# The last norm of a two-block transformer kernel: a shorter root, factors moved from GpSimd to VectorE, stores in four pieces

## Chip, core and metric

The kernel runs as one program on one core of a Trainium2 chip. The metric is the device time of one execution in microseconds; the median of three runs is compared. Engines are named as the profile names them: PE is TensorE (matmul), PEld its weight loads, DVE is VectorE, ACT is ScalarE, POOL is GpSimd, SP is SyncE, which here only issues transfers.

## What is computed

Two transformer blocks are applied to 256 tokens of width 1024, the first with two layers of attention, the second with a feed-forward net (ffn), a mixer, a second ffn, a gated projection and the last norm. Only the end matters here:

```python
h = h + 0.5 * swiglu(rms_norm_2(h, ffn2_norm[i]), ffn2_w_in[i], ffn2_w_out[i])
hn = rms_norm_2(h, ple_norm[i])
h = h + jax.nn.sigmoid(hn @ ple_w_gate[i]) * (p[i] @ ple_w_proj[i])
return rms_norm_2(h, final_norm)        # x * rsqrt(mean(x*x) + EPS) * g
```

## The kernel before

All weights are one stream of chunks of 8 tiles of 128x128. SP loads a chunk into `wraw` (4 buffers; line 97), ACT rounds it into `whi` (line 108), DVE computes the rest `wlo` (line 115), and PE multiplies with both (line 86). The instructions of each engine stand in the order in which the program writes them; nothing reorders them at run time, so an instruction that waits holds up all that stand behind it on its engine. `tick` is called once a chunk: it starts the split of the chunk two ahead and lets side tasks take one step each.

A norm (`Norm.stats`) is such a side task. PE sums squares into a PSUM bank, POOL sets a small tile `nv` to 1.0 (line 354), DVE writes the mean squares into that same tile (line 361), takes a reciprocal root in 11 small instructions (lines 284 to 289), and PE spreads the result over the partitions (line 315, and line 86 for its last part). Since DVE's write comes after POOL's in the same tile, DVE waits for POOL. The norm in front of the second ffn is called `fstats`.

Between `fstats` being spawned and the second ffn the program makes pool `q4`, and SP loads the last norm's factors `gf` into it, one copy a partition (line 1582).

The last part takes the 1024 columns in cuts of 512, 256 and 256 (`PLE_CUT`), for two halves `i` of 128 tokens each. For each cut and half the generator `finals` multiplies by the gate (line 1619), adds the residual (line 1621), sums squares in ACT (line 1622) and multiplies by `gf` (line 1625): in DVE, but for the last cut of the second half in POOL. Then `rsqrt1` takes the root of one column of numbers by a bit trick (line 297) and three steps of two instructions (lines 299 and 300); after the second step of the first half's root DVE does the second half's gate and residual (`between`). The rows are then scaled by the root and stored: of the second half, ACT scales 384 columns (line 1674) and DVE 640 (line 1676), and each queue stores its part in one transfer (lines 1677 and 1678).

Of the kernel before, what the change touches and what calls it, by code (L numbers as in the profile page):

```python
# [14 lines left out]
AF = mybir.ActivationFunctionType  # L15
OP = mybir.AluOpType
# [7 lines left out]
P = 128  # L24
# [33 lines left out]
def hybrid_kernel(ctx: ExitStack, tc: tile.TileContext, wst, xt, pt, gains, c0, c1, c2, lmaskc, alpha, relb, rpb, gfin, out):  # L58
    nc = tc.nc
    V, S, G, PE = nc.vector, nc.scalar, nc.gpsimd, nc.tensor  # L60
# [6 lines left out]
    def nm(s):  # L67
        count[0] += 1
        return f"{s}_{count[0]}"

    def act(w=NT, dt=F32, p=P):

        assert w <= NT
        return sb.tile([P, TP], dt, tag="a", name=nm("a"), bufs=A_BUFS)[:p, :w]

    def til(shape, tag, bufs=1, dt=F32, pool=None):
        return (pool or sb).tile(shape, dt, tag=tag, name=nm(tag), bufs=bufs)

    def bank(tag):
        return ps.tile([P, 512], F32, tag=tag, name=nm(tag), bufs={"mm": 3, "at": 4, "st": 1}[tag])  # L80
# [120 lines left out]
    def finish(*names):  # L201
        while any(n not in done for n in names) or pending:
            tick()
# [36 lines left out]
    def proj(acts, n, evac, need=None, work=1):  # L240

        b = bank("mm")[:, :n]
        last = len(acts) - 1
        for k in range(last + 1):
            xh, xl = acts[k]
            wh, wl = weights(1)
            mm(b, wh, xh[:, :n], start=k == 0, stop=False)
            mm(b, wh, xl[:, :n], start=False, stop=False)
            mm(b, wl, xh[:, :n], start=False, stop=k == last)
            if k == last:  # L250
                pending.append([evac, b, need, work])
            used()

    def triple(b, hl, wts, i, first, last):

        t = slice(i * P, (i + 1) * P)
        mm(b, hl[0][:, t], wts[0], start=first, stop=False)
        mm(b, hl[1][:, t], wts[0], start=False, stop=False)
        mm(b, hl[0][:, t], wts[1], start=False, stop=last)

    def split(x, scale, n=NT, pool=None):

        if pool:
            hi, lo = til([P, n], "hid", 44, F32R, pool), til([P, n], "hid", 44, F32R, pool)
        else:
            hi, lo = act(n, F32R), act(n, F32R)
        split_into((hi, lo), x, scale)
        return hi, lo
# [24 lines left out]

    def rsqrt1(m, mh, between=()):

        y, t = til([P, 1], "nyf", 2, pool=q4), til([P, 1], "ntf", 2, pool=q4)
        V.tensor_scalar(y.bitcast(I32), m.bitcast(I32), -0.5, float(0x5F3759DF), op0=OP.mult, op1=OP.add)
        for k in range(3):
            V.scalar_tensor_tensor(t, y, mh, y, op0=OP.mult, op1=OP.mult)
            V.scalar_tensor_tensor(y, t, 1.5, y, op0=OP.add, op1=OP.mult)  # L300
            if k == 1:
                for f in between:
                    f()
        return y

    def bcast(cols, b, rows=False):
# [133 lines left out]
    norm = Norm(gn[:, G_NORM:], NT)  # L440
# [46 lines left out]
    for l in range(2):  # L487
        t = dr.tile([P, pitch], F32, name=f"rows{l}")
# [524 lines left out]
    nxt = Norm(gn[:, G_NORM + 8:], NT)  # L1013
# [3 lines left out]
    norm, nxt = nxt, Norm(g2, NR, gn[:, G_FIN1:])  # L1017
# [5 lines left out]
    norm, nxt = nxt, Norm(gn[:, G_MIX:], NR)  # L1023
# [11 lines left out]
    def ffn(norm, nxt, pad=0):  # L1035
        hl = norm.hl
        fs = ExitStack()
        q2 = fs.enter_context(tc.tile_pool(name=nm("q2"), bufs=1))
        if pad:
            til([P, pad], "padf", pool=q2)  # L1040
        hid, zs = [], []

        def ev_g(b):
            z = act(NR)
            V.tensor_tensor(z, b, norm.rb, op=OP.mult)  # L1045
            S.activation(z, z, AF.Silu)  # L1046
            zs.append(z)

        def ev_u(b):
            z = zs.pop(0)  # L1050
            V.tensor_tensor(z, b, z, op=OP.mult)  # L1051
            hid.append(split(z, 0.5, NR, q2))

        for j in range(22):
            proj(hl, NR, ev_g, norm.ready)
            proj(hl, NR, ev_u)
        for j in range(8):
            def ev(b, j=j):
                x = act(NR)
                V.tensor_tensor(x, b, norm.rb, op=OP.mult)  # L1060
                V.tensor_tensor(x, x, norm.xs[j], op=OP.add)  # L1061
                nxt.add(x)
            proj(hid, NR, ev)
        finish()
        fs.close()

    ffn(norm, nxt, 32)
    norm, nxt = nxt, Norm(gn[:, G_FFN2:], NR)
# [509 lines left out]
    norm, nxt = nxt, Norm(gn[:, G_PLE:], NR)  # L1578
    spawn("fstats", norm.stats(rows=True))
    q4 = ctx.enter_context(tc.tile_pool(name="q4", bufs=1))  # L1580
    gf = q4.tile([P, 1024], F32, name="gf")
    nc.sync.dma_start(gf, bass.AP(tensor=gfin.tensor, offset=gfin.offset, ap=[[0, P], [1, 1024]]))
    til([P, 32], "pad2")
    ffn(norm, nxt, 16)
    norm = nxt

    turned = [[bank("at") for _ in range(2)] for _ in range(2)]
# [23 lines left out]
    os_ = [til([P, 1024], "fo", 2, pool=q4) for _ in range(2)]  # L1611

    def finals(wp, i, c, o, w):
        b = bank("mm")[:, :w]
        for k in range(2):
            triple(b, phl[k], [x[:, k * w:(k + 1) * w] for x in wp], i, k == 0, k == 1)
        t = os_[i][:, o:o + w]
        yield
        V.scalar_tensor_tensor(t, t, 1.0, b, op0=OP.add, op1=OP.mult)
        yield  # L1620
        V.tensor_tensor(t, t, turned[i][o // 512][:, o % 512:o % 512 + w], op=OP.add)
        S.activation(til([P, 512], "fsq", 2, pool=q4)[:, :w], t, AF.Square, scale=1.0 / 32,
                     accum_out=su[:, 2 * c + i:2 * c + i + 1])
        yield
        (G if c == 2 and i else V).tensor_tensor(t, t, gf[:, o:o + w], op=OP.mult)  # L1625
        yield

    assert pos[0] == MOVED
    for c, (o, w) in enumerate(PLE_CUT):
        bs = [bank("mm")[:, :w] for _ in range(2)]  # L1630
        if c < 2:
            d = CH * P // w
            for k in range(0, 8, d):
                wts = [weights(w // P) for _ in range(d)]
                for i in range(2):
                    for j in range(d):
                        triple(bs[i], norm.hl[k + j], wts[j], i, k + j == 0, k + j == 7)
                used()
            if c == 0:
                finish("plestats", "turn")  # L1640
            for i in range(2):
                S.activation(os_[i][:, o:o + w], bs[i], AF.Tanh, scale=hr[:, i:i + 1])
            wp = weights(2 * w // P)
            fs = [finals(wp, i, c, o, w) for i in range(2)]
            for n in (1, 2):
                for f in fs:
                    for _ in range(n):
                        next(f)
            used()
            for f in fs:  # L1650
                next(f)
        else:
            V.scalar_tensor_tensor(sv, su[:, :2], EPS, su[:, 2:4], op0=OP.add, op1=OP.add)
            V.tensor_scalar(svh, sv, -0.5, None, op0=OP.mult)
            wts = [weights(w // P) for _ in range(8)]
            wp = weights(2 * w // P)
            fs = [finals(wp, i, c, o, w) for i in range(2)]
            for i in range(2):
                for k in range(8):
                    triple(bs[i], norm.hl[k], wts[k], i, k == 0, k == 7)  # L1660
                S.activation(os_[i][:, o:o + w], bs[i], AF.Tanh, scale=hr[:, i:i + 1])
                next(fs[i])
                if i == 0:
                    next(fs[0]), next(fs[0])
            for i in range(2):
                next(fs[i])
                v, vh = til([P, 1], "fv", 2), til([P, 1], "fvh", 2, pool=q4)
                V.tensor_tensor(v, sv[:, i:i + 1], su[:, 4 + i:5 + i], op=OP.add)
                V.scalar_tensor_tensor(vh, su[:, 4 + i:5 + i], -0.5, svh[:, i:i + 1], op0=OP.mult, op1=OP.add)
                r = rsqrt1(v, vh, () if i else [lambda: next(fs[1])] * 2)  # L1670
                t = slice(i * P, (i + 1) * P)
                cut = 384 if i else 512
                a, b = os_[i][:, :cut], os_[i][:, cut:]
                S.activation(a, a, AF.Copy, scale=r)
                if i:
                    V.tensor_scalar(b, b, r, None, op0=OP.mult)
                    S.dma_start(out[t, :cut], a)
                    nc.sync.dma_start(out[t, cut:], b)
                else:
                    nc.sync.dma_start(out[t, :cut], a)  # L1680
                    S.activation(b, b, AF.Copy, scale=r)
                    S.dma_start(out[t, cut:], b)
    assert pos[0] == n_chunk * CH, (pos[0], wst.shape)


# [152 lines left out]
```

## Time and profile before

| | |
|---|---|
| median of 3 runs | 1072.31 us (1071.44 to 1072.75) |
| the profiled execution's own time | 1072.28 us |
| its span in the trace | 1070.5 us |
| granted clock of TensorE over the span | 0.998 |
| PE busy | 1059.7 us (99%) |
| DVE busy | 796.4 us (74%) |
| ACT busy | 585.5 us (55%) |
| POOL busy | 53.9 us (5%) |

Times in the trace count from the start of the span. The execution's own time is 1.8 us longer than its span, and 0.03 us from the median. A matmul's row counts as busy while it is queued, so a PE of 99% says little of its speed; whether it is held up is read from the starts of its instructions.

### The profile page before, as it was taken

Reading aid. Unit: us, or ns where it says so; the run is one execution under the profiler, and the core shown is the slowest. Engines: PE = TensorE matmul, PEld = TensorE weight load, DVE = VectorE, ACT = ScalarE, POOL = GpSimd, SP = SyncE. Lnnn points to the kernel's source line nnn. Section 1 sums busy time; section 2 is a strip of 40 time slices with the busy share of each in tenths; the row PEclk is TensorE's granted clock in tenths of the full one; section 3 lists DMA queues with packets and bytes.
Section 4 is the critical chain, followed back from the end, with each engine's and each line's share of the span. In section 5 each row is a group of like instructions: output and inputs, shape, how many; then the busy total and the mean of one; then the engine's idle time right before and its main releaser. Section 6 shows DMA issues by size and latency. Waiting matters only on the chain.

```text
span 1070.5 us, 22921 instructions
## 1 busy us (share of the span) xinstructions
PE 1059.7 (99%) x9183; PEld 1020.9 (95%) x9183; DVE 796.4 (74%) x1646; ACT 585.5 (55%) x1035; POOL 53.9 (5%) x111
## 2 busy tenths in 40 slices
PE   9999999999999999999999999999999999999996
PEld 8999899999999999999999987999999999999996
DVE  7888867788887788766666659996687866666666
ACT  7356644544565466555545475777554655554444
POOL 3420002012000000000000200000000000000000
PEclk9999999999999999999999999999999999999999
DMA  8763345565434565655665535544455665556651
GB/s 291 230 209 120 121 137 167 188 171 180 150 122 137 172 192 166 207 195 195 196 212 186 189 130 178 178 139 139 138 183 194 208 189 195 196 197 197 200 175 59
DMA packets 71900, 188.08 MB, mean 176 GB/s; under 512 B 22745, under 2 KB 27353, under 8 KB 71794
## 3 DMA queue, kind: packets, MB, share of 16 engines
q1 hardware_dynamic: 71362, 186.12, 53.6%
q8 instruction: 72, 1.18, 0.5%
q10 hardware_dynamic: 432, 0.50, 0.1%
q14 instruction: 34, 0.28, 0.1%
HBM read 185.53 MB, written 3.65 MB: 177 GB/s over the span
## 4 chain that ended last, share of the span: by engine, by line
PE 92%; DVE 5%; DMA 1%; issue 1%; ACT 0%; SPq 0%; POOL 0%; DVEq 0%; ACTq 0%
PE mm L86 82%; PE at L86 7%; DVE wlo L115 2%; DMA wraw<-in_wst_dram 1%; PE at L752 1%; PE st L86 1%; DVE sc L1221 1%; DVE m L1220 0%; PE at L819 0%; PE st L315 0%; ACT whi L108 0%; PE at L820 0%; PE at L821 0%; DVE fo L1625 0%; SPq L431 0%
## 5 line engine op out<-in xcount | busy, mean ns | idle before, releaser
L86 PE MATMUL mm<-a,whi 128*128 128x256 f32 (+1 forms) x4192 | 747.1, 282 | 0.0
L86 PEld LDWEIGHTS mm<-a,whi 128*128 128x128 f32 x4192 | 637.7, 188 | 7.2 <-issue 5.6
L86 PE MATMUL mm<-a,wlo 128*128 128x256 f32 (+1 forms) x2096 | 585.2, 279 | 0.0
L115 DVE TENSOR_TENSOR wlo<-wraw,whi 128x1024 fp32r<-128x1024 f32 (+1 forms) x341 | 411.0, 1208 | 19.0 <-ACT whi L108 18.0
L86 PEld LDWEIGHTS mm<-a,wlo 128*128 128x128 f32 x2096 | 394.0, 188 | 0.0
L108 ACT ACTIVATE whi<-wraw 128x1024 fp32r<-128x1024 f32 (+1 forms) x341 | 354.5, 1042 | 67.6 <-PE mm L86 46.1
L86 PE MATMUL mm<-hid,whi 128*128 128x256 f32 x704 | 119.8, 276 | 0.0
L86 PEld LDWEIGHTS mm<-hid,whi 128*128 128x128 f32 x704 | 105.9, 188 | 0.0
L86 PE MATMUL mm<-hid,wlo 128*128 128x256 f32 x352 | 97.2, 276 | 0.0
L86 PEld LDWEIGHTS mm<-hid,wlo 128*128 128x128 f32 x352 | 66.1, 188 | 0.0
L1051 DVE TENSOR_TENSOR a<-mm,a 128x256 f32<-128x256 f32 x42 | 17.8, 424 | 46.4 <-PE mm L86 46.4
L271 ACT ACTIVATE hid<-a 128x256 fp32r<-128x256 f32 x44 | 18.5, 421 | 57.0 <-DVE a L1051 57.0
L86 PE MATMUL mm<-whi,a 128*128 128x512 f32 (+1 forms) x184 | 46.7, 346 | 0.0
L1046 ACT ACTIVATE a<-a 128x256 f32<-128x256 f32 x44 | 18.4, 418 | 49.5 <-DVE a L1045 49.4
L271 ACT ACTIVATE a<-a,gn 128x256 fp32r<-128x256 f32 (+1 forms) x40 | 20.6, 514 | 43.9 <-DVE a L1061 25.9
L1045 DVE TENSOR_TENSOR a<-mm,rb 128x256 f32<-128x256 f32 x42 | 17.8, 424 | 27.5 <-PE mm L86 27.5
L86 PEld LDWEIGHTS mm<-whi,a 128*128 128x128 f32 x184 | 31.0, 188 | 4.3 <-issue 0.3
L409 ACT ACTIVATE gate<-gate 128x272 f32<-128x272 f32 (+1 forms) x32 | 13.6, 424 | 38.8 <-DVE gate L408 38.8
L533 ACT ACTIVATE pra<-at,mx,hs 128x272 f32<-128x272 f32 x32 | 18.2, 573 | 28.6 <-DVE mx L700 28.6
L1060 DVE TENSOR_TENSOR a<-mm,rb 128x256 f32<-128x256 f32 x16 | 6.8, 425 | 34.4 <-PE mm L86 34.4
L86 PE MATMUL mm<-wlo,a 128*128 128x512 f32 (+1 forms) x92 | 31.5, 342 | 0.0
L271 ACT ACTIVATE a<-a 128x256 fp32r<-128x256 f32 (+1 forms) x24 | 10.1, 422 | 26.4 <-DVE a L1564 12.1
(339 smaller groups left out, 1030.7 us busy)
## 6 DMA issues: line engine op xcount, KB each, us to landing
wraw<-in_wst_dram SPq DMA_DIRECT2D x332, 512.0 KB, 3.7
bias<-rows SPq DMA_DIRECT2D x16, 160.0 KB, 4.3
rows<-in_rpb_dram SPq DMA_DIRECT2D x8, 316.0 KB, 5.3
wraw<-in_wst_dram SPq DMA_DIRECT2D x8, 256.0 KB, 4.4
a<-in_xt_dram SPq DMA_DIRECT2D x8, 136.0 KB, 4.3
big<-tb SPq DMA_DIRECT2D x2, 512.0 KB, 5.2
c<-in_c_dram SPq DMA_DIRECT2D x1, 512.0 KB, 4.3
gf<-in_gfin_dram SPq DMA_DIRECT2D x1, 512.0 KB, 4.7
```

Of the source, the lines that this page charges most:

```text
L86: PE.matmul(o, l, r, start=start, stop=stop)
L108: S.activation(his[c][:, s], raws[c][:, s], AF.Copy)
L115: V.tensor_tensor(los[c][:, s], raws[c][:, s], his[c][:, s].bitcast(F32), op=OP.subtract)
L271: S.activation(hl[0], x, AF.Copy, scale=scale)
L409: S.activation(t, t, AF.Tanh, scale=0.5)
L533: S.activation(outs[i], src, AF.Exp, bias=bias, scale=scale, accum_out=su[:, i:i + 1])
L752: PE.transpose(b[:, j * P:(j + 1) * P], pr[:, o:o + P], ident)
L1045: V.tensor_tensor(z, b, norm.rb, op=OP.mult)
L1046: S.activation(z, z, AF.Silu)
L1051: V.tensor_tensor(z, b, z, op=OP.mult)
L1060: V.tensor_tensor(x, b, norm.rb, op=OP.mult)
L1221: V.match_replace(sc[:, w], m8, sc[:, w], TAKEN)
```

## The change

The root of the last norm takes one step of third order (three instructions on the column) and one of second order (two) in place of three of second order. Both new steps leave out a constant factor, 1.5 and 2.25, together 3.375, so POOL multiplies `gf` by 3.375 once, ahead of the second ffn. The last cut of the second half is no longer multiplied by `gf` in POOL: DVE does it together with the scaling by the root. The second half is scaled and stored in four pieces: 256 columns by DVE with the factors and 384 by DVE without, both stored from SP's queue, and twice 192 by ACT, stored from ACT's queue. A pad of 16 numbers in the ffn's pool goes; the new small tile `nuf` takes the room, and no other tile has another address.

```diff
     def rsqrt1(m, mh, between=()):
-        y, t = til([P, 1], "nyf", 2, pool=q4), til([P, 1], "ntf", 2, pool=q4)
+        y, t, u = [til([P, 1], f"n{c}f", 2, pool=q4) for c in "ytu"]
         V.tensor_scalar(y.bitcast(I32), m.bitcast(I32), -0.5, float(0x5F3759DF), op0=OP.mult, op1=OP.add)
-        for k in range(3):
-            V.scalar_tensor_tensor(t, y, mh, y, op0=OP.mult, op1=OP.mult)
-            V.scalar_tensor_tensor(y, t, 1.5, y, op0=OP.add, op1=OP.mult)
-            if k == 1:
-                for f in between:
-                    f()
+        V.scalar_tensor_tensor(t, y, mh, y, op0=OP.mult, op1=OP.mult)
+        V.scalar_tensor_tensor(u, t, 5 / 3, t, op0=OP.add, op1=OP.mult)
+
+        V.scalar_tensor_tensor(y, u, 1.25, y, op0=OP.add, op1=OP.mult)
+        for f in between:
+            f()
+        V.scalar_tensor_tensor(t, y, mh, y, op0=OP.mult, op1=OP.mult)
+        V.scalar_tensor_tensor(y, t, 2 / 3, y, op0=OP.add, op1=OP.mult)
         return y
...
     til([P, 32], "pad2")
-    ffn(norm, nxt, 16)
+    G.tensor_scalar(gf, gf, 3.375, None, op0=OP.mult)
+    ffn(norm, nxt)
...
-        (G if c == 2 and i else V).tensor_tensor(t, t, gf[:, o:o + w], op=OP.mult)
+        if c < 2 or i == 0:
+            V.tensor_tensor(t, t, gf[:, o:o + w], op=OP.mult)
...
-                cut = 384 if i else 512
-                a, b = os_[i][:, :cut], os_[i][:, cut:]
-                S.activation(a, a, AF.Copy, scale=r)
+                x = os_[i]
                 if i:
-                    V.tensor_scalar(b, b, r, None, op0=OP.mult)
-                    S.dma_start(out[t, :cut], a)
-                    nc.sync.dma_start(out[t, cut:], b)
+                    V.scalar_tensor_tensor(x[:, o:], x[:, o:], r, gf[:, o:], op0=OP.mult, op1=OP.mult)
+                    nc.sync.dma_start(out[t, o:], x[:, o:])
+                    V.tensor_scalar(x[:, 384:o], x[:, 384:o], r, None, op0=OP.mult)
+                    nc.sync.dma_start(out[t, 384:o], x[:, 384:o])
+                    for s in (slice(0, 192), slice(192, 384)):
+                        S.activation(x[:, s], x[:, s], AF.Copy, scale=r)
+                        S.dma_start(out[t, s], x[:, s])
```

The first place is POOL's queue from the mixer to the end. Here are its rows before, with what each waits for; `nv_11651` is the small tile of `fstats`, `nv_13966` that of the next norm, `fo_13950` the second half's rows.

```order
L1357 MEMSET big_8805 128x1024
L1109 CAST lmask_8159<-a_8157 128x192 [waits DMAHW1_49]
L354 MEMSET nv_11651 128x4
L354 MEMSET nv_13966 128x4 [waits DVE_49]
L1625 TENSOR_TENSOR fo_13950<-fo_13950,gf 128x256 [waits DMAHW3_49,DMAHW4_49,DMAHW0_49,DMAHW6_49,PE_49,DMAHW7_49,Activation_49,Pool_49]
```

And the same rows now (its line numbers are those of the changed kernel, here 3 higher).

```order
L1360 MEMSET big_8805 128x1024
L1112 CAST lmask_8159<-a_8157 128x192 [waits DMAHW1_49]
L1587 TENSOR_SCALAR gf<-gf 128x1024 [waits DMAHW3_49,DMAHW0_49,DMAHW4_49,DVE_49,DMAHW6_49,PE_49,DMAHW7_49,Activation_49,Pool_49]
L357 MEMSET nv_11651 128x4
L357 MEMSET nv_13966 128x4
```

The scaling of `gf`, which waits for the load of `gf` among others, now stands ahead of the MEMSET of the small tile of `fstats`, which waited for nothing; the multiplication at the end is gone.

The second place is DVE's queue at `fstats`, as it is now, with what each row waits for; its order is the same as before.

```order
L343 TENSOR_TENSOR sqacc_11327<-sqacc_11327,a_11606 128x256 [waits Activation_49]
L364 TENSOR_SCALAR nv_11651<-st_11650 128x2 [waits PE_49,Pool_49]
L284 TENSOR_SCALAR nyv_11658<-nv_11651 128x4 [waits DVE_49]
...
L289 SCALAR_TENSOR_TENSOR nyv_11658<-ntv_11659,nyv_11658 128x4 [waits DVE_49]
L115 TENSOR_TENSOR wlo_11672<-wraw_11490,whi_11655 128x1024 [waits DMAHW7_49,Activation_49]
L115 TENSOR_TENSOR wlo_11705<-wraw_11530,whi_11701 128x1024 [waits DMAHW0_49,Activation_49]
```

The first small instruction of `fstats` (line 361 before, 364 now) waits for PE's sums and for POOL's MEMSET, and two weight splits stand behind its root.

The third place is DVE's last instructions, the second half's root and scaling; before:

```order
L297 TENSOR_SCALAR nyf_14271<-fv_14267 128x1
L299 SCALAR_TENSOR_TENSOR ntf_14272<-nyf_14271,fvh_14268 128x1
L300 SCALAR_TENSOR_TENSOR nyf_14271<-ntf_14272,nyf_14271 128x1
L299 SCALAR_TENSOR_TENSOR ntf_14272<-nyf_14271,fvh_14268 128x1
L300 SCALAR_TENSOR_TENSOR nyf_14271<-ntf_14272,nyf_14271 128x1
L299 SCALAR_TENSOR_TENSOR ntf_14272<-nyf_14271,fvh_14268 128x1
L300 SCALAR_TENSOR_TENSOR nyf_14271<-ntf_14272,nyf_14271 128x1
L1676 TENSOR_SCALAR fo_13950<-fo_13950,nyf_14271 128x640
```

And now:

```order
L298 TENSOR_SCALAR nyf_14270<-fv_14266 128x1
L299 SCALAR_TENSOR_TENSOR ntf_14271<-nyf_14270,fvh_14267 128x1
L300 SCALAR_TENSOR_TENSOR nuf_14272<-ntf_14271 128x1
L302 SCALAR_TENSOR_TENSOR nyf_14270<-nuf_14272,nyf_14270 128x1
L305 SCALAR_TENSOR_TENSOR ntf_14271<-nyf_14270,fvh_14267 128x1
L306 SCALAR_TENSOR_TENSOR nyf_14270<-ntf_14271,nyf_14270 128x1
L1679 SCALAR_TENSOR_TENSOR fo_13950<-fo_13950,nyf_14270,gf 128x256
L1681 TENSOR_SCALAR fo_13950<-fo_13950,nyf_14270 128x384
```

Of the seven instructions of the root six are left, and the one scaling of 640 columns has become one of 256 with the factors and one of 384.

## Rows read from the trace of the kernel before

**Rows 1.** Page, parts 4 and 5: chain that ended last; weight loads, mean ns.

```profile
PE 92%; DVE 5%; DMA 1%; issue 1%; ACT 0%; SPq 0%; POOL 0%; DVEq 0%; ACTq 0%
...
L86 PEld LDWEIGHTS mm<-a,whi 128*128 128x128 f32 x4192 | 637.7, 188 | 7.2 <-issue 5.6
```

**Rows 2.** Chain that ended last, in order of time: start, us, what.

```profile
860.57 171.57 PE mm L86 x1512
```

**Rows 3.** Timeline of the end, all engines: start, us, instruction, idle before.

```profile
1061.67 0.47 ACT L1661 ACTIVATE fo<-mm,hr 128x256 f32<-128x256 f32 x1 [0.71 <-PE mm L86]
...
1062.04 0.28 PE L86 MATMUL mm<-wlo,a 128*128 128x256 f32 x1
...
1062.50 0.42 DVE L1619 SCALAR_TENSOR_TENSOR fo<-fo,mm 128x256 f32<-128x256 f32 x1
...
1063.80 0.19 ACT L1622 ACTIVATION_READ_ACCUMULATOR fsq<-fo 128x1 f32 x1
...
1064.12 0.73 POOL L1625 TENSOR_TENSOR fo<-fo,gf 128x256 f32<-128x256 f32 x1 [298.79 <-ACT fsq L1622]
...
1064.40 0.46 DVE L299 SCALAR_TENSOR_TENSOR ntf<-nyf,fvh 128x1 f32<-128x1 f32 x1
...
1065.54 0.22 DVE L299 SCALAR_TENSOR_TENSOR ntf<-nyf,fvh 128x1 f32<-128x1 f32 x1
1065.79 0.16 DVE L300 SCALAR_TENSOR_TENSOR nyf<-ntf,nyf 128x1 f32<-128x1 f32 x1
1065.99 0.61 ACT L1674 ACTIVATE fo<-fo,nyf 128x384 f32<-128x384 f32 x1 [0.78 <-DVE nyf L300]
1066.06 0.55 DVE L1676 TENSOR_SCALAR fo<-fo,nyf 128x640 f32<-128x640 f32 x1
1066.63 0.37 ACTq L1677 DMA_DIRECT2D out_dram<-fo  x1
1066.64 0.34 SPq L1678 DMA_DIRECT2D out_dram<-fo  x1
```

**Rows 4.** Transfers of the last 7.5 us: size, us from issue to landing.

```profile
out_dram<-fo SPq DMA_DIRECT2D x1, 256.0 KB, 2.0
...
out_dram<-fo ACTq DMA_DIRECT2D x1, 192.0 KB, 2.8
```

**Rows 5.** Load of the factors: SP's timeline, and page part 6.

```profile
853.37 0.38 SPq L1582 DMA_DIRECT2D gf<-in_gfin_dram  x1
...
gf<-in_gfin_dram SPq DMA_DIRECT2D x1, 512.0 KB, 4.7
```

**Rows 6.** POOL's timeline: instructions of several kinds and sizes.

```profile
62.70 2.98 POOL L522 TENSOR_TENSOR bias<-c,bias 128x1280 f32<-128x1280 f32 x1 [10.14 <-DMA bias<-rows]
...
167.45 0.96 POOL L497 TENSOR_SCALAR rot<-c,gn 128x272 f32<-128x272 f32 x1
...
601.17 1.25 POOL L1133 TENSOR_SCALAR sc<-c 128x256 f32<-128x256 f32 x1
...
604.05 1.86 POOL L1357 MEMSET big<- 128x1024 f32 x2
...
606.14 0.10 POOL L354 MEMSET nv<- 128x4 f32 x1
```

**Rows 7.** DVE's timeline at `fstats`.

```profile
854.49 0.16 DVE L361 TENSOR_SCALAR nv<-st 128x2 f32<-128x2 f32 x1 [0.83 <-PE st L86]
...
856.47 0.16 DVE L289 SCALAR_TENSOR_TENSOR nyv<-ntv,nyv 128x4 f32<-128x4 f32 x1
856.55 2.36 DVE L115 TENSOR_TENSOR wlo<-wraw,whi 128x1024 fp32r<-128x1024 f32 x2
```

**Rows 8.** PE's timeline at the spreading of the root.

```profile
859.77 0.27 PE L315 MATMUL st<-c,nyv 128*128 128x128 f32 x1
...
860.83 0.28 PE L86 MATMUL mm<-a,wlo 128*128 128x256 f32 x1
```

**Rows 9.** Busy time of each engine in one stretch; PEclk is the granted clock.

```profile
1030.00:1040.00 10.00, 9.85 (x59) 8.28 (x59) 6.63 (x19) 4.25 (x6) 0.00 (x0) 1.00 0.32 107
```

More of the change, by code (lines that the diff above doesn't have):

```diff
@@ L1671, in hybrid_kernel @@
                 t = slice(i * P, (i + 1) * P)
-                cut = 384 if i else 512
-                a, b = os_[i][:, :cut], os_[i][:, cut:]
-                S.activation(a, a, AF.Copy, scale=r)
+                x = os_[i]
                 if i:
-                    V.tensor_scalar(b, b, r, None, op0=OP.mult)
-                    S.dma_start(out[t, :cut], a)
-                    nc.sync.dma_start(out[t, cut:], b)
-                else:
-                    nc.sync.dma_start(out[t, :cut], a)
-                    S.activation(b, b, AF.Copy, scale=r)
-                    S.dma_start(out[t, cut:], b)
+                    V.scalar_tensor_tensor(x[:, o:], x[:, o:], r, gf[:, o:], op0=OP.mult, op1=OP.mult)
[5 more added lines that the diff above has]
+                        S.dma_start(out[t, s], x[:, s])
+                else:
+                    for s, q in ((slice(0, 512), nc.sync), (slice(512, 1024), S)):
+                        S.activation(x[:, s], x[:, s], AF.Copy, scale=r)
+                        q.dma_start(out[t, s], x[:, s])
     assert pos[0] == n_chunk * CH, (pos[0], wst.shape)
```

## The prediction

> **What bounds the kernel now.** I first read the page's chain that ended last: PE has 92% of it and DVE 5% [rows 1]. So a change is worth something only where PE waits or where no PE work is left, and I looked for both. The chain in order of time shows that from the start of the second ffn PE works through 171.57 us without a gap [rows 2]: a stall put in front of this stretch moves everything behind it, and nothing there takes it up again. The timeline of the end shows PE's last matmul at 1062.04 [rows 3]; from there on the kernel is a chain of DVE, ACT and the stores, about 8 us long. The change touches it there, and in one other place that the diff does not make plain: POOL's queue ahead of the second ffn.
>
> **What the end gains.** All in the timeline of the end [rows 3].
>
> 1. Root of the first half. A pair of lines 299 and 300 takes 0.22 and 0.16 us and starts 0.25 and 0.20 us apart (1065.54 to 1065.79, and 0.04 from the end at 1065.95 to the next start at 1065.99). One pair, 0.45 us, gives way to one more instruction of line 300's kind, 0.20, so DVE would come to the second half's gate (1062.50) 0.25 us earlier, at 1062.25. But that reads PE's last product, done at 1062.04 + 0.28 = 1062.32; with 0.04 for the start it begins at 1062.36. Gain 0.14 us, and the squares, their sum and the second root follow.
> 2. POOL's multiplication ran from 1064.12 to 1064.85, and in it the first instruction of the second root took 0.46 us in place of the 0.22 of the same line at 1065.54. With POOL idle I take 0.24 back (0 if that was not POOL's doing).
> 3. The second root saves the same pair: 0.25 us.
>
> The root, ready at 1065.79 + 0.16 = 1065.95, should be ready 0.63 us earlier, relative to PE.
>
> 4. Scaling and stores. Before, the last store is issued 0.68 us after the root (1066.63) and lands 2.8 us later [rows 4], at 3.48 us after the root. A single store of 256 KB takes 2.0 us and the two that share 512 KB take 2.8 [rows 4], so I count 0.8 us for every 256 KB and 1.2 us fixed. Now ACT scales 192 columns (at most the 0.47 us that 256 take at 1061.67; I take 0.45), issues (0.37), scales again, issues again: the first store leaves 0.52 us after the root and the last 1.40 us, later than the 0.68 of before. All 512 KB behind a first issue at 0.52 end at 0.52 + 1.2 + 1.6 = 3.32; the last 96 KB alone would end at 1.40 + 1.5 = 2.9, so the transfer rate decides. Gain 0.16 us; at best 0.58. On DVE the 256 columns with factors (0.42 us as in the same instruction at 1062.50) and the 384 (below the 0.55 of the 640) both end before ACT's second piece, so they don't decide.
>
> Together 0.79 us; from 0.39 (POOL not to blame, stores no faster) to 1.2.
>
> **What POOL's queue costs.** Before, the MEMSET of the small tile of `fstats` ran at 606.14 [rows 6], 248 us before DVE needed it. Now the scaling of `gf` stands ahead of it and waits for the load of `gf`. SP issues that at 853.37 and it lands 4.7 us later, at 858.07 [rows 5]. DVE's first instruction of `fstats` started at 854.49 [rows 7], so DVE now waits for POOL. Step by step:
>
> - POOL starts 0.15 us after the landing: it took 0.13 us from the end of ACT's sum (1063.99) to POOL's start (1064.12) [rows 3]. 858.22.
> - The scaling itself, 1024 columns by a constant, is on no row. The nearest are the same operation with 272 columns, 0.96 us with little beside it, and with 256 columns and two constants, 1.25 us beside a busy DVE [rows 6]. For the 752 further columns: a MEMSET, which only writes, takes 1.86 / 2 = 0.93 us for 1024, or 0.91 ns a column; a TENSOR_TENSOR, which reads two tiles, takes 0.73 us for 256 [rows 3] and 2.98 for 1280 [rows 6], or 2.2 ns a column. So 0.96 + 0.68 = 1.64 to 0.96 + 1.65 = 2.61. The lowest bound is the MEMSET's whole 0.93 (no fixed part), the highest the 272 columns scaled up, 3.6. I take 1.75: one tile read and one written is nearer to the MEMSET, and DVE is idle then, so nothing competes.
> - The MEMSET, 0.10 us. DVE starts at 858.22 + 1.75 + 0.10 = 860.07, which is 5.58 us late.
> - The root's last instruction ended at 856.47 + 0.16 = 856.63 [rows 7]; now 862.21. PE's spreading takes the root as weights, so a weight load of 0.19 us [rows 1] comes between: 862.21 + 0.03 + 0.19 = 862.43. In the trace PE reached it at 859.77 [rows 8], 3.14 us after the root was there. That was the cover; what is left is a stall of 2.66 us.
> - Behind the waiting instruction on DVE stand two weight splits. The first started at 856.55 and, half of the two's 2.36 us, ended about 857.75 [rows 7]; now 863.33, loaded as weights by 863.55. PE wants it at 860.83 + 2.66 = 863.49 [rows 8]: 0.06 us more. The second is wanted a whole chunk later and is in time. SP's next chunk load waits for the first of these splits, so it goes out 5.6 us later, but PE is 2.7 us later too and that chunk is needed four chunks on, over 10 us; I cost this at nothing. If loads were late there, PE would lose up to 2.9 us more.
>
> PE loses 2.72 us. The clock I leave alone: in the stretch from 1030 to 1040 PE issued 59 matmuls where the long stretch has 88 in 10 us (1512 in 171.57 [rows 2]), so it stood for some 3 us, and its granted clock stayed at 1.00, the level of 2.4 GHz [rows 9].
>
> Here the Trainium skill can be weighed against the trace. The row of 272 columns takes 3.5 ns a column if it is scaled up [rows 6], and with that the total would be 1076.1. The GPSIMD Engine Reference, section 4.1 (Engine selection), calls one-input elementwise work on GpSimd "roughly line-rate", and section 3.1 gives 1.03 cycles an element for short bodies and 1.8 for a tight unrolled loop at 1.2 GHz. By an estimate from that page the scaling takes 0.88 to 1.54 us, and the total would be 1073.3 to 1074.0. No run so far shows which is right.
>
> **Sum.** 2.72 - 0.79 = +1.9 us on the profiled execution's 1072.28 us; the median of 1072.31 is the same within 0.03. Forecast 1074.2 us, +0.18%. A measurement of this kernel can tell about 0.2%, 2.14 us, from no change, so I forecast a slowdown just under what counts.
>
> **Rivals.**
>
> - *POOL's scaling is slower than 1.96 us.* Then the stall passes 2.93 us and the sum 2.14: slower. At 2.61 us the total is 1075.1, at 3.6 us 1076.1. For it: 272 columns took 0.96 us, and two reads cost 2.2 ns a column. Against: the MEMSET's rate. Chance 0.41.
> - *The stall does not reach PE.* If the `gf` load landed some 3 us earlier, or PE had more cover, only the end's gain would be left: 1072.28 - 0.79 = 1071.5. Against it: landing, MEMSET and cover are rows, and the wait stands in DVE's queue. Chance 0.04, and it still counts as the same.
> - *The four stores end later than the two.* ACT's second piece is issued 1.40 us after the root against 0.68; should each small store cost its own 2.0 us or more and not 1.5, the last lands at 1.40 + 2.0 to 2.4 = 3.4 to 3.8 us, and of the 0.79 some 0.3 to 0.7 are left: 1074.3 to 1074.7. By itself this changes no verdict; it lowers the point of the first rival to 1.5 us at worst.
> - *Forecast*: scaling between 0.93 and 1.96 us, 1073.4 to 1074.4. Chance 0.53.
>
> **How the numbers follow.** Low end: scaling 0.93 (stall 1.90) and gain 1.2, +0.7, 1073.0. High end: scaling 2.61 (stall 3.58) and gain 0.39, +3.2, 1075.5. Outside lie the hidden stall and the scaling of 3.6, together under 2 in 10. Faster by 0.2% needs 1070.1, which no case reaches: 0.02 for what I don't see. Slower 0.41, within 0.2% 0.57.
>
> **What would show it.** Right: POOL's scaling of `gf` starts near 858.2 and takes about 1.75 us; DVE's first instruction of `fstats` starts near 860.1 with idle time put down to POOL; PE's spreading starts near 862.4, and all of PE behind it is 2.7 us late up to its last matmul near 1064.8; the first instruction of the second root takes 0.22 us; the root is ready 3.0 us after the end of PE's last matmul (3.63 before) and the last store lands 3.3 us after that. Wrong: a spreading at 859.8 (no stall), a scaling over 2 us, a stall with further gaps in the following chunks, or a last store later than 3.5 us after the root.

## The result: slower by 0.53%, a pause of PE and a lower clock behind it

The changed kernel took 1077.93 us (median of 4 runs, 1076.16 to 1079.32) against 1072.38 for the kernel before: ratio 1.0053, 95% interval 1.0041 to 1.0065. 1074.2 us was forecast, with a range up to 1075.5. The place of the loss was forecast, its size was not. The profiled execution, whose rows follow, took 1076.16 us, the lowest of the four.

POOL's timeline of the changed kernel at the second ffn (start, us, instruction, idle before and its releaser):

```profile
857.05 2.77 POOL L1587 TENSOR_SCALAR gf<-gf 128x1024 f32<-128x1024 f32 x1 [251.59 <-DMA gf<-in_gfin_dram]
859.77 0.14 POOL L357 MEMSET nv<- 128x4 f32 x2
```

The MEMSET that ran at 606.14 before [rows 6] now comes behind a wait of 251.59 us for the load of `gf` and 2.77 us of scaling. DVE's timeline at `fstats`:

```profile
859.90 0.16 DVE L364 TENSOR_SCALAR nv<-st 128x2 f32<-128x2 f32 x1 [7.54 <-POOL nv L357]
...
861.87 0.16 DVE L289 SCALAR_TENSOR_TENSOR nyv<-ntv,nyv 128x4 f32<-128x4 f32 x1
```

DVE stood 7.54 us for that MEMSET; in [rows 7] it waited 0.83 us, for PE. The chain of work that ended last, in order of time (start, us, what), goes through the same names:

```profile
852.08 4.54 DMA gf<-in_gfin_dram
...
856.64 0.04 POOLq L1587
...
857.05 2.77 POOL gf L1587
...
862.18 0.29 PE st L318
862.47 0.53 PE st L86 x4
863.01 173.26 PE mm L86 x1512
...
1047.22 19.74 PE mm L86 x144
```

The load of `gf` and POOL, which are not in this part of the chain before, now stand in front of PE's spreading (L318). And the 1512 matmuls behind it take 173.26 us, where they took 171.57 [rows 2]. The busy times by stretch say why; the column behind POOL's is the granted clock:

```profile
860.00:862.50 2.50, 0.32 (x3) 0.35 (x3) 2.15 (x12) 0.00 (x0) 0.00 (x0) 1.00 0.00 0
862.50:863.50 1.00, 1.00 (x8) 0.86 (x8) 1.00 (x2) 0.44 (x2) 0.00 (x0) 1.00 0.00 0
863.50:864.00 0.50, 0.50 (x5) 0.50 (x5) 0.50 (x1) 0.50 (x1) 0.00 (x0) 0.73 0.00 0
864.00:865.00 1.00, 1.00 (x7) 1.00 (x6) 0.65 (x2) 0.99 (x2) 0.00 (x0) 0.50 0.85 180
...
866.00:867.00 1.00, 1.00 (x6) 1.00 (x6) 1.00 (x2) 1.00 (x3) 0.00 (x0) 0.50 0.82 266
...
868.00:869.00 1.00, 1.00 (x11) 1.00 (x10) 1.00 (x2) 0.83 (x2) 0.00 (x0) 1.00 0.78 147
```

PE stood until 862.18, worked on at 1.00 for about 1.5 us, and then got 0.50 of its clock, 1.2 in place of 2.4 GHz, until about 867. The end, in the timeline of all engines:

```profile
1066.67 0.28 PE L86 MATMUL mm<-wlo,a 128*128 128x256 f32 x1
...
1068.95 0.22 DVE L299 SCALAR_TENSOR_TENSOR ntf<-nyf,fvh 128x1 f32<-128x1 f32 x1
...
1069.84 0.16 DVE L306 SCALAR_TENSOR_TENSOR nyf<-ntf,nyf 128x1 f32<-128x1 f32 x1
1070.04 0.48 DVE L1679 SCALAR_TENSOR_TENSOR fo<-fo,nyf,gf 128x256 f32<-128x256 f32 x1
1070.17 0.46 ACT L1684 ACTIVATE fo<-fo,nyf 128x192 f32<-128x192 f32 x1 [0.42 <-DVE nyf L306]
...
1071.53 0.34 ACTq L1685 DMA_DIRECT2D out_dram<-fo  x1
```

The root is ready at 1070.00, 3.05 us after PE's last matmul ended at 1066.95 (3.63 before [rows 3]). The span of 1074.4 us ends 7.45 us after that matmul, where the 1070.5 us of before end 8.18 us after theirs: the end did gain, 0.73 us. Of the four stores of the second half the two of ACT stand in the list of transfers as:

```profile
out_dram<-fo ACTq DMA_DIRECT2D x2, 96.0 KB, 2.0
```

The head of the second ffn needs one more reference point, PE's sums of `fstats`, which nothing in the change touches. They stand in PE's timeline of the changed kernel at

```profile
852.51 0.58 PE L86 MATMUL st<-c,sqacc 128*128 128x1 f32 x4
```

and in that of the kernel before at

```profile
853.80 0.58 PE L86 MATMUL st<-c,sqacc 128*128 128x1 f32 x4
```

so the profiled execution of the changed kernel had a head start of 1.29 us there.

### The profile page after: what moved, and what is told of

It reads as the page before. It is cut to its first block, busy times and chain, and to the rows that moved or that the text cites. A ratio compares the mean times of both kernels' runs of the same rounds, so it can differ in the third digit from the quotient of the medians.

```text
span 1074.4 us, 22923 instructions
## 1 busy us (share of the span) xinstructions
PE 1061.4 (99%) x9183; PEld 1022.8 (95%) x9183; DVE 793.9 (74%) x1645; ACT 585.6 (55%) x1036; POOL 57.2 (5%) x111
## 4 chain that ended last, share of the span: by engine, by line
PE 95%; DVE 3%; DMA 1%; ACT 0%; issue 0%; POOL 0%; SPq 0%; ACTq 0%; POOLq 0%; DVEq 0%
PE mm L86 84%; PE at L86 8%; DVE wlo L115 1%; PE at L755 1%; PE st L86 1%; DVE sc L1224 1%; DMA wraw<-in_wst_dram 0%; DMA gf<-in_gfin_dram 0%; DVE m L1223 0%; PE at L822 0%; PE st L318 0%; POOL gf L1587 0%; PE at L824 0%; PE at L823 0%; DVE big L1341 0%
```

## The experiments

Each was compared with the kernel before on the same chip: 1071.93 us in the first group (the first four), 1071.8 in the second (the last four).

**The scaling behind the ffn** (x1_late).

```diff
-    G.tensor_scalar(gf, gf, 3.375, None, op0=OP.mult)
     ffn(norm, nxt)
+    G.tensor_scalar(gf, gf, 3.375, None, op0=OP.mult)
```

> The changed kernel with POOL's scaling of gf written behind the second ffn, so that the MEMSET of fstats stands ahead of it in POOL's queue again. Theory A (POOL's order holds up DVE and then PE, and the fall of TensorE's clock after that pause is the rest): DVE's first instruction of fstats starts within 0.2 us of PE's sums again, PE's spreading has no idle time before it, no stretch at 0.5 of the clock behind it, and the total is the kernel before less what the end gains, 0.6 to 0.9 us: 1071.5 to 1071.8. POOL then scales beside DVE's work; if that costs PE anything it is under 1 us. Rival B (another part of the change, the end's or the pad's, costs the time): 1076 or more. Rival C (the stall goes but the lower clock stays, since it comes from something else): 1073 to 1074.

Measured: 1071.36 us, ratio 0.9995 (0.9982 to 1.0007). The two lines in the other order take the whole loss away: it is 0.57 us below the kernel before. Its chain in order of time:

```profile
859.60 0.11 PE st L318
859.71 0.53 PE st L86 x4
860.24 171.59 PE mm L86 x1512
...
1042.78 19.23 PE mm L86 x144
```

No wait ahead of the spreading, and the long stretch takes 171.59 us again. POOL still scales, now beside DVE:

```profile
857.83 3.17 POOL L1588 TENSOR_SCALAR gf<-gf 128x1024 f32<-128x1024 f32 x1 [252.10 <-DMA gf<-in_gfin_dram]
```

It takes 0.4 us longer there, and PE does not notice.

**The scaling alone** (x2_scale_only): the kernel before, which multiplies `gf` by 1.0 at that place.

```diff
+    G.tensor_scalar(gf, gf, 1.0, None, op0=OP.mult)
     ffn(norm, nxt, 16)
```

> The kernel before with one instruction added: POOL multiplies gf by 1.0 where the change multiplies it by 3.375; root, factors and stores as before. Theory A: DVE waits for POOL as in the changed kernel, PE's spreading comes 3.7 us late, the clock falls to 0.5 for some 3 us after it, and the total is the changed kernel's plus what its end had gained: 1078.4 to 1078.8 (+6). Rival B (the end costs the time): 1072.4. Rival C (stall without the lower clock): 1076.

Measured: 1078.13 us, ratio 1.0060 (1.0047 to 1.0072): one instruction that changes no number costs 6.2 us. Its chain:

```profile
863.10 0.29 PE st L315
863.39 0.53 PE st L86 x4
863.92 173.26 PE mm L86 x1512
```

The spreading waited 3.58 us for DVE here (3.54 in the changed kernel), and the stretch behind it takes the same 173.26 us. Rival B, that the end costs the time, is out, and so is C, the stall without the lower clock.

**A quarter of the scaling** (x3_quarter).

```diff
-    G.tensor_scalar(gf, gf, 3.375, None, op0=OP.mult)
+    G.tensor_scalar(gf[:, :256], gf[:, :256], 3.375, None, op0=OP.mult)
     ffn(norm, nxt)
+    G.tensor_scalar(gf[:, 256:], gf[:, 256:], 3.375, None, op0=OP.mult)
```

> The changed kernel with only 256 of the 1024 columns of gf scaled ahead of the ffn and the other 768 behind it. Theory A with a scaling whose time goes by columns: the first piece takes about 0.9 us in place of 2.77, PE's stall is 3.7 - 1.9 = 1.8 us. If the clock does not fall after this pause: 1072.4 + 1.8 - 0.6 = 1073.6. If it falls as long as in the changed kernel: 1.7 more, 1075.3. Rival (scaling is mostly a fixed cost): the piece takes over 2 us and the total stays near 1077.5.

Measured: 1074.82 us, ratio 1.0035 (1.0018 to 1.0053). POOL's timeline:

```profile
857.64 0.85 POOL L1587 TENSOR_SCALAR gf<-gf 128x256 f32<-128x256 f32 x1 [251.52 <-DMA gf<-in_gfin_dram]
...
858.50 2.13 POOL L1589 TENSOR_SCALAR gf<-gf 128x768 f32<-128x768 f32 x1
```

So POOL multiplies a column in (2.77 - 0.85) / 768 = 2.5 ns and has a fixed 0.21 us; the 768 columns fit this with 0.21 + 1.92 = 2.13 us. PE's timeline and its chain:

```profile
861.27 0.29 PE L318 MATMUL st<-c,nyv 128*128 128x128 f32 x1 [2.12 <-DVE nyv L289]
```

```profile
862.10 173.28 PE mm L86 x1512
```

The pause is longer than the 1.8 us expected, and the rows show it on DVE: the second instruction of `fstats` took 0.58 us here, beside POOL's other 768 columns, and 0.17 us in the changed kernel, where POOL has nothing to do by then (here first, the changed kernel below it).

```profile
858.77 0.58 DVE L284 TENSOR_SCALAR nyv<-nv 128x4 int32<-128x4 int32 x1
```

```profile
860.10 0.17 DVE L284 TENSOR_SCALAR nyv<-nv 128x4 int32<-128x4 int32 x1
```

In the profiled execution (1075.27 us) a pause of 2.12 us was followed by the same loss of 1.7 us. But three of the six executions took 1073.74 to 1074.37 us with a mean granted clock of 0.998 or 0.999, and two 1075.27 and 1075.92 with 0.997 and 0.996 (the sixth took 1081.31 with 0.996, which nothing here explains). So it seems that both halves of the expectation came true, 1073.6 without the lower clock and 1075.3 with it, in different executions of one kernel. Only the profiled one shows its stretches. The others show this by time and mean clock alone, and a mean also holds the end of the span, where PE has no work left and the clock is lower in every profile: z2_root_only below has 0.997, and its clock does not fall before PE's last matmul.

**PE kept at work during the wait**, at first (x4_fill) ahead of every spreading that shares its code path.

```diff
             def pe():
+                if rows:
+                    f, h = bank("at"), self.hl[0][0]
+                    for _ in range(29):
+                        mm(f[:, :NR], h[:, :P], h)
                 bcast([self.rc[:, i:i + 1].to_broadcast([P, P]) for i in range(nt)], bb,
```

> The changed kernel with 29 matmuls of 256 columns, 3.3 us of work whose result nobody reads, put on PE just ahead of the spreading of fstats, where PE stands idle for 3.5 us in the changed kernel. Theory A in two parts, stall and clock apart: the spreading comes as late as in the changed kernel (3.7 us), the granted clock stays at 1.00, and the total is 1.7 us or more below the changed kernel: 1075.5 to 1076. Rival (the lower clock does not come from PE's standing): no gain, 1077.9 or a little more.

Measured: 1084.99 us. This edit was too wide: another norm, far ahead, takes the same branch, and PE's sums of `fstats` began some 10 us later than in the other runs (863.22). The total says nothing of the question, but its chain does: with PE at work during the wait the stretch of 1512 matmuls takes 171.66 us in it. The edit was done again for `fstats` alone (x5_fill), by an argument `fill=29` that only its `stats` gets in place of `if rows`.

> The changed kernel with 29 matmuls of 256 columns whose result nobody reads on PE just ahead of the spreading of fstats, this time of that norm alone. Stall and clock apart: the spreading comes as late as in the changed kernel, but PE works until then, the granted clock stays at 1.00 and the stretch behind it takes 171.6 us in place of 173.3. Total 1.7 to 2.5 us below the changed kernel's 1077.9: 1075.4 to 1076.2. Rival (the clock falls for another reason than PE's standing): 1077.9 or more.

Measured: 1075.12 us (7 runs, 1074.82 to 1075.62 but for one of 1081.65), ratio 1.0040 (1.0024 to 1.0056). That is 3.3 us above the kernel before on its chip, where the changed kernel is 5.55 above: 2.2 us less. Its chain:

```profile
859.82 3.48 PE at L86 x29
863.36 0.29 PE st L318
863.66 0.53 PE st L86 x4
864.19 171.64 PE mm L86 x1512
...
1046.78 19.23 PE mm L86 x144
```

And the stretch in which the clock would have fallen:

```profile
864.00:868.00 4.00, 4.00 (x35) 3.93 (x35) 3.45 (x6) 3.25 (x6) 0.00 (x0) 1.00 0.60 179
```

The delay is the same, 9.68 us from PE's sums of `fstats` (853.68) to the spreading (9.67 in the changed kernel); the clock stays at 1.00 and the stretch takes 171.64 us. More work on PE gave a faster kernel.

**No scaling at all** (y1_fold). 32 times 3.375 is 108, so the constant can go into the squares:

```diff
-    G.tensor_scalar(gf, gf, 3.375, None, op0=OP.mult)
...
-        S.activation(til([P, 512], "fsq", 2, pool=q4)[:, :w], t, AF.Square, scale=1.0 / 32,
+        S.activation(til([P, 512], "fsq", 2, pool=q4)[:, :w], t, AF.Square, scale=1.0 / 108,
...
-            V.scalar_tensor_tensor(sv, su[:, :2], EPS, su[:, 2:4], op0=OP.add, op1=OP.add)
+            V.scalar_tensor_tensor(sv, su[:, :2], EPS / 3.375 ** 2, su[:, 2:4], op0=OP.add, op1=OP.add)
```

> The changed kernel without POOL's scaling of gf at all: the 3.375 is put into the squares instead (their scale 1/108 in place of 1/32, EPS divided by 3.375 squared), where it costs no instruction. Theory A: as with the scaling behind the ffn, no wait for POOL, no fall of the clock, the end's gain kept: 1071.2 to 1071.6, 0.5 to 0.9 below the kernel before. Rival (POOL's scaling beside DVE's work costs something even where PE does not stand): some 0.3 us or more below the run with the scaling behind the ffn.

Measured: 1070.82 us (11 runs, 1069.91 to 1071.65) against 1071.8 (30 runs): ratio 0.9992, 0.9983 to 1.0001. This is the version that keeps what the end gains: 0.98 us below the kernel before, a little more than the 0.5 to 0.9 expected, where the changed kernel is 5.55 above. That it beats the kernel before is likely, but the interval just takes in no change. Whether the 0.4 us to x1_late, which is 0.57 below, is POOL's scaling or chance these runs can't tell.

**Two stores in place of four** (z1_two_stores), on y1_fold:

```diff
-                    nc.sync.dma_start(out[t, o:], x[:, o:])
                     V.tensor_scalar(x[:, 384:o], x[:, 384:o], r, None, op0=OP.mult)
-                    nc.sync.dma_start(out[t, 384:o], x[:, 384:o])
-                    for s in (slice(0, 192), slice(192, 384)):
-                        S.activation(x[:, s], x[:, s], AF.Copy, scale=r)
-                        S.dma_start(out[t, s], x[:, s])
+                    nc.sync.dma_start(out[t, 384:], x[:, 384:])
+                    S.activation(x[:, :384], x[:, :384], AF.Copy, scale=r)
+                    S.dma_start(out[t, :384], x[:, :384])
```

> The kernel with the folded factor, second half stored in two pieces again (DVE 256 with factors and 384 without, one store of 640 columns; ACT 384 columns, one store). Theory (four pieces gain 0.16 us): the last store lands 3.5 us after the root, the span ends 0.1 to 0.2 us later than with four pieces, 1071.4 to 1071.8. Rival (the split matters more): 0.4 us or more later.

Measured: 1071.47 us, ratio 0.9996 (0.9987 to 1.0005). The end of its timeline, and its transfers (size, us from issue to landing):

```profile
1065.46 0.16 DVE L306 SCALAR_TENSOR_TENSOR nyf<-ntf,nyf 128x1 f32<-128x1 f32 x1
...
1066.50 0.34 SPq L1680 DMA_DIRECT2D out_dram<-fo  x1
```

```profile
out_dram<-fo SPq DMA_DIRECT2D x1, 320.0 KB, 2.7
```

The last store lands at 1066.50 + 2.7 = 1069.2, 3.6 us after the root (1065.62), and the span of 1070.3 ends 4.7 us after it. In the changed kernel the last of four is issued 1.53 us after the root (1071.53 against 1070.00), lands 2.0 us after its issue, 3.5 us after the root, and the span ends 4.4 us after it. So in these profiles four pieces gain hardly anything at the landing (the 2.0 is the median of two stores) and 0.3 us at the end of the span; in the totals the 0.65 us between z1_two_stores and y1_fold is within both kernels' spread.

**The root alone** (z2_root_only): the kernel before with the new `rsqrt1`, the folded constant of y1_fold and the pad removed.

> The kernel before with the new root alone (folded factor, POOL's multiplication and two stores as before). Theory: the second half's root is ready 3.2 to 3.3 us after the end of PE's last matmul (3.63 before): 0.14 us from the first root, 0.25 from the second, while the second root's first instruction beside POOL still takes 0.46 us. Total 1071.6 to 1072.0. Rival (POOL is not what slows that instruction): it takes 0.22 us.

Measured: 1071.35 us, ratio 0.9996 (0.9988 to 1.0005). Its timeline:

```profile
1062.55 0.28 PE L86 MATMUL mm<-wlo,a 128*128 128x256 f32 x1
...
1064.55 0.72 POOL L1628 TENSOR_TENSOR fo<-fo,gf 128x256 f32<-128x256 f32 x1 [299.44 <-ACT fsq L1625]
...
1064.83 0.46 DVE L299 SCALAR_TENSOR_TENSOR ntf<-nyf,fvh 128x1 f32<-128x1 f32 x1
...
1065.97 0.16 DVE L306 SCALAR_TENSOR_TENSOR nyf<-ntf,nyf 128x1 f32<-128x1 f32 x1
```

The root is ready 1066.13 - 1062.83 = 3.30 us after PE's last matmul, inside what was expected (the total is 0.25 us below the range expected), and beside POOL the one instruction takes 0.46 us again, against 0.22 at 1068.95 in the changed kernel. The 0.24 us was POOL's doing.

## Why the prediction was wrong, step by step

**The mechanism of POOL's queue was right, two of its terms were too small.** Measured from PE's sums of `fstats` to its spreading, the distance grew from 859.77 - 853.80 = 5.97 us to 862.18 - 852.51 = 9.67: PE lost 3.70 us where 2.66 were forecast.

- "I take 1.75" for the scaling of 1024 columns: it took 2.77, and this is 1.02 of the 1.04 us. The step behind it, "one tile read and one written is nearer to the MEMSET", fails: 2.5 ns a column against the MEMSET's 0.91, and no less than the 2.2 of two tiles read. The row of the same operation with 272 columns was the right guide, if its 0.96 us had been read as mostly columns: 0.21 + 272 x 2.5 ns = 0.89. The Trainium skill, GPSIMD Engine Reference, section 4.1 (Engine selection), calls one-input work "roughly line-rate", and its section 3.1 (Elementwise — side-by-side cycle accounting) has 1.03 cycles an element for short bodies and 1.8 for a tight loop at 1.2 GHz, by an estimate 0.88 to 1.54 us here. The measurement decides against it: 2.77 us with DVE idle. By an estimate from the 1.2 GHz of the same page of the Trainium skill, 2.5 ns would be 3 cycles.
- "POOL starts 0.15 us after the landing": the landing at 852.08 + 4.54 = 856.62 and the start at 857.05 are 0.43 apart. The instruction's waits take four steps of POOL's queue, and the chain has all four behind the landing, the first at 856.64. The 0.13 us of L1625 did not hold them: it has four such steps too, but three of them had passed by 858.3, after `gf` had landed, and only the last waited for ACT's sum. This is 0.28 us more; the load landed 0.16 us earlier relative to PE's sums than before, and PE's weight load took 0.15 and not 0.22 us, which takes it back.
- The two weight splits behind the waiting instruction cost next to nothing, as forecast (0.06), and the later chunk loads nothing: x5_fill has the whole delay and its stretch takes 171.64 us.

**"The clock I leave alone" was the other step that failed, and it rested on a misread row.** The prediction took the 59 matmuls between 1030 and 1040 [rows 9] for a sign that PE "stood for some 3 us". But most matmuls there move 512 columns and not 256. Between the two rows below lie the starts of three of them, in 0.70 us; three of 256 columns take 0.34 us (171.57 us for 1512):

```profile
1039.96 0.63 PE L86 MATMUL mm<-whi,a 128*128 128x512 f32 x2
...
1040.66 0.63 PE L86 MATMUL mm<-whi,a 128*128 128x512 f32 x2
```

No two matmuls there start more than 0.54 us apart (1034.53 to 1035.07), and only one part of the stretch is not wholly busy, by 0.15 us:

```profile
1034.00:1036.00 2.00, 1.85 (x10) 1.32 (x10) 1.13 (x5) 1.83 (x2) 0.00 (x0) 1.00 0.39 96
```

So these rows show nothing about a pause of 2.7 us. The trace of the kernel before had another place that bears on it: behind PE's last matmul, which ends at 1062.32, PE stands and the clock falls to 0.50.

```profile
1064.00:1066.00 2.00, 0.00 (x0) 0.00 (x0) 1.73 (x9) 1.22 (x3) 0.73 (x1) 1.00 0.27 101
1066.00:1068.00 2.00, 0.00 (x0) 0.00 (x0) 0.55 (x1) 0.60 (x1) 0.00 (x0) 0.66 0.68 259
1068.00:1070.00 2.00, 0.00 (x0) 0.00 (x0) 0.00 (x0) 0.00 (x0) 0.00 (x0) 0.50 0.43 164
```

That was reason enough to give the clock a term with a chance of its own in place of nothing. In the changed kernel it fell, and the long stretch lost 173.26 - 171.57 = 1.69 us. That PE's standing is the cause is shown by x5_fill, in which PE has work during the same delay and the clock stays.

**In the profiled execution the 144 matmuls from 1047.22 on took 19.74 us**, 0.51 more than in x1_late, y1_fold, z1_two_stores and x5_fill (19.23). No term of the sum had this. x2_scale_only and x3_quarter, whose clock fell too, have 19.74, but so has z2_root_only, whose clock did not fall. So it does not need the fall; what it is, and whether the fall brings it on, stays open.

**The end gained what was forecast, in part by luck**: 0.73 us in the profiles against 0.79. The root came 0.58 us earlier relative to PE (0.63 forecast), of which 0.24 is POOL's multiplication gone and 0.33 the shorter root (z2_root_only, 3.63 to 3.30, where 0.39 were forecast). The span ends 4.40 us after the root and not 4.55, which is 0.15 us for the stores where 0.16 were forecast, but not for the reason given. The last store was to land 3.32 us after the root; it landed at 3.5, as before. Each store of 96 KB took 2.0 us and not 1.5, which is the condition of the rival in which the four stores end later. The 0.15 us lies between the last landing and the end of the span, and what shortens it stays open.

The parts add up. In the two profiled executions 3.70 + 1.69 + 0.51 - 0.73 = 5.17 us, and 0.04 for the split; less the head start of 1.29 us the spans should differ by 3.92 us, and do by 3.9. The change puts nothing ahead of that point, so I take the head start as the executions' own. The medians differ by 5.55 us; the 0.3 us that are left are well inside the spread of the four runs.

Of the rivals, "POOL's scaling is slower than 1.96 us" was the one that cost time, with its own 1075.1 at 2.61 us still 2.8 us short: no case had the clock in it.

## What to carry to other kernels

An instruction put at the head of an idle engine's queue brings its wait to everything written behind it there, however small: look for who on another engine waits for those, even where the engine is 95% idle and its next use is far away. Before an instruction is costed by its kind, take the row of the same operation on the same engine and ask how much of it goes by columns. A stall of PE has two prices, the pause and what the clock may do behind it, and the second, as the times of x3_quarter suggest, is partly chance: take both ends into the range, and where the stall can't be avoided, PE can be given something to do. Before a count of matmuls is read as idle time, look at their shapes.

## What was not expected of the hardware

- One kernel (x3_quarter) ran at two speeds, 1073.7 to 1074.4 and 1075.3 to 1075.9 us, with mean clocks of 0.998 to 0.999 and 0.996 to 0.997; its profile, of one of the slower, has a pause of 2.12 us and a fall of the clock behind it.
- POOL's one-input multiplication by a constant costs 2.5 ns a column (0.85 us for 256 columns, 2.77 for 1024), more than its two-input TENSOR_TENSOR (2.2 ns a column).
- An instruction of POOL whose waits take four steps of its queue started 0.43 us after the landing that released it where all four steps came behind the landing, and 0.13 us after its releaser where only the last one did.
- The same 144 matmuls of the last part take 19.23 or 19.74 us in different profiled executions, at a granted clock of 1.00 in both.
